# A softmax kernel: the first chunk's store split into a 512-byte head and the rest

## The chip, the cores and the metric

The kernel runs on one core of one Trainium2 chip. The metric is the device time of one execution in microseconds. Before the change it is 161.81 us, the median of three runs (161.65 to 161.95).

## The reference

A softmax with temperature 0.5 over the last dimension of a float32 tensor of 16 x 1024 x 512:

```python
temp = 0.5
x_scaled = x / temp
x_max = np.max(x_scaled, axis=-1, keepdims=True)
exp_x = np.exp(x_scaled - x_max)
return exp_x / np.sum(exp_x, axis=-1, keepdims=True)
```

33.55 MB are read and 33.55 MB are written; there is no matrix product.

## The kernel before

The 16384 rows are cut into 8 chunks of 2048 rows. A chunk is a tile `xt` of 128 partitions x 16 rows x 512 values, so each partition holds 16 neighbouring rows, one contiguous run of 32768 bytes in memory. All work on a chunk is done in place in this tile. There are six buffers (`BUFS`), so chunk 6 takes the buffer of chunk 0 and chunk 7 that of chunk 1, and their loads wait until those chunks are stored.

*Loads* (L61 to L69) are issued by SP on its queue, q1. Chunk 0 comes in two parts (rows 0 to 3, then 4 to 15), chunks 1 to 6 whole, and of chunk 7 the first 15 rows. The loads of chunks 0 to 5 go out one after the other at the start; those of 6 and 7 wait for a store. The last row of chunk 7 is loaded by POOL (L88 to L100, queue q0) after an exponential of chunk 5.

*Blocks* are what the engines work on: chunk 0 in three blocks (rows 0 to 3, 4 to 7, 8 to 15), chunk 7 in two halves, the others whole; eleven in all. For each block:
- `shift` (L71 to L81): DVE takes the negated maximum of each row (L77) and doubles it as a bias (L81);
- `exponentials` (L102 to L117): ACT computes exp(2x + bias) for one row of every partition per instruction (L108) and sums it up on the way;
- `scale_vector` (L120 to L131): DVE takes the reciprocals (L125) and multiplies the first 7/8 of the block's rows (L127);
- `scale_scalar` (L133 to L142): ACT multiplies the other eighth, row by row (L138);
- `store` (L144 to L152): when a chunk's last block is scaled, ACT issues one DMA of the whole chunk on its queue, q10 (L148). The table `STORES` has one whole store per chunk.

The order is written out by hand (L154 to L172), with a manual schedule. In step i, ACT runs the exponentials of block i+1, then DVE and ACT scale block i, then DVE shifts block i+2, then ACT issues the store. For block 3 (chunk 1) two of its 16 exponentials are kept back and run after the store that stands before them on ACT, which is chunk 0's store (L159, L172). The names of the DMAs are collected in `finished`; a last instruction on SP (L174) waits for them.

Below, load 5 or store 0 is that of chunk 5 or 0.

Of the kernel before, what the change touches and what calls it, by code (L numbers as in the profile page):

```python
# [1 line left out]

# [4 lines left out]


@with_exitstack
def kernel(  # L10
    ctx: ExitStack,
    tc: tile.TileContext,
    x: bass.AP,
    out: bass.AP,
):
    nc = tc.nc
    fp32 = mybir.dt.float32
    P = nc.NUM_PARTITIONS
    AX = mybir.AxisListType.X
    EXP = mybir.ActivationFunctionType.Exp  # L20
    COPY = mybir.ActivationFunctionType.Copy
    MAX = mybir.AluOpType.max

    D = x.shape[-1]
    xf = x.flatten_outer_dims()
    of = out.flatten_outer_dims()
    N = xf.shape[0]

    G = 16
    C = N // (P * G)
    assert C * P * G == N
    xr = xf.rearrange("(c p g) d -> c p g d", p=P, g=G)
    outr = of.rearrange("(c p g) d -> c p g d", p=P, g=G)
    WHOLE = [(0, G)]
    LOADS = [[(0, 4), (4, G)]] + [WHOLE] * 6 + [[(0, G - 1)]]
    BLOCKS = [[(0, 4), (4, 8), (8, G)]] + [WHOLE] * 6 + [[(0, 8), (8, G)]]
    STORES = [WHOLE] * 8  # L40
    BMAX = 16
    BUFS = 6

    data = ctx.enter_context(tc.tile_pool(name="data", bufs=BUFS))
    stats = ctx.enter_context(tc.tile_pool(name="stats", bufs=6))

    ctx.enter_context(tc.manual_schedule())


    warm = stats.tile([P, 1], fp32, name="warm", bufs=1)  # L50
    nc.vector.memset(warm, 0.0)  # L51
    nc.scalar.activation(out=warm, in_=warm, func=EXP)  # L52

    chunks = {}
    blocks = [(c, lo, hi) for c in range(C) for lo, hi in BLOCKS[c]]
    n = len(blocks)
    biases, sums, recips = {}, {}, {}

    finished = []

    def load(c):  # L61
        if c < BUFS:
            chunks[c] = data.tile([P, G, D], fp32, name="xt")
        else:
            chunks[c] = chunks[c - BUFS]
        xt = chunks[c]
        for lo, hi in LOADS[c]:
            part = nc.sync.dma_start(out=xt[:, lo:hi, :], in_=xr[c][:, lo:hi, :])  # L68
            finished.append(part.ins.name)  # L69

    def shift(i):  # L71
        c, lo, hi = blocks[i]
        if c not in chunks:
            load(c)
        b = hi - lo
        negmax = stats.tile([P, BMAX], fp32, name="negmax")
        nc.vector.tensor_reduce(  # L77
            negmax[:, 0:b], chunks[c][:, lo:hi, :], axis=AX, op=MAX, negate=True
        )
        biases[i] = stats.tile([P, BMAX], fp32, name="bias")  # L80
        nc.vector.tensor_scalar_mul(biases[i][:, 0:b], negmax[:, 0:b], 2.0)  # L81

    def load_last_row(signal):  # L88
        seen = stats.tile([P, 1], fp32, name="seen", bufs=1)
        copied = nc.gpsimd.tensor_copy(out=seen, in_=signal)  # L90
        finished.append(copied.ins.name)
        c = C - 1
        halves = "p (h d) -> p h d"
        to = chunks[c - BUFS][:, G - 1, :].rearrange(halves, h=2)
        of_ = xr[c][:, G - 1, :].rearrange(halves, h=2)
        for p0, p1 in ((P - 2, P), (0, P - 2)):
            part = nc.gpsimd.dma_start(  # L97
                out=to[p0:p1], in_=of_[p0:p1], max_dma_last_dim=2 * D
            )
            finished.append(part.ins.name)  # L100

    def exponentials(i, rows):  # L102
        c, lo, hi = blocks[i]
        if i not in sums:
            sums[i] = stats.tile([P, BMAX], fp32, name="sums")
        for g in rows:
            row = chunks[c][:, lo + g, :]
            nc.scalar.activation(  # L108
                out=row,
                in_=row,  # L110
                func=EXP,
                bias=biases[i][:, g : g + 1],
                scale=2.0,
                accum_out=sums[i][:, g : g + 1],
            )
            if c == BUFS - 1 and g == 10:
                load_last_row(sums[i][:, g : g + 1])  # L117


    def scale_vector(i):  # L120
        c, lo, hi = blocks[i]
        b = hi - lo
        k = b - b // 8
        recips[i] = stats.tile([P, BMAX], fp32, name="recip")
        nc.vector.reciprocal(recips[i][:, 0:b], sums[i][:, 0:b])  # L125
        rows = chunks[c][:, lo : lo + k, :]
        last = nc.vector.tensor_mul(  # L127
            rows, rows, recips[i][:, 0:k].unsqueeze(2).broadcast_to((P, k, D))
        )
        if i == n - 1:  # L130
            finished.append(last.ins.name)  # L131

    def scale_scalar(i):  # L133
        c, lo, hi = blocks[i]
        b = hi - lo
        for g in range(b - b // 8, b):
            row = chunks[c][:, lo + g, :]
            last = nc.scalar.activation(  # L138
                out=row, in_=row, func=COPY, scale=recips[i][:, g : g + 1]
            )  # L140
            if i == n - 1:
                finished.append(last.ins.name)  # L142

    def store(i):  # L144
        c, _, end = blocks[i]
        for lo, hi in STORES[c]:
            if hi == end:
                part = nc.scalar.dma_start(  # L148
                    out=outr[c][:, lo:hi, :], in_=chunks[c][:, lo:hi, :]
                )  # L150
                if c < C - 1:
                    finished.append(part.ins.name)  # L152

    shift(0)  # L154
    shift(1)

    def rows(i):
        c, lo, hi = blocks[i]
        cut = hi - lo - (2 if c == 1 else 0)  # L159
        return range(cut), range(cut, hi - lo)  # L160

    exponentials(0, rows(0)[0])
    for i in range(n):
        if i + 1 < n:
            exponentials(i + 1, rows(i + 1)[0])
        scale_vector(i)
        scale_scalar(i)
        if i + 2 < n:
            shift(i + 2)
        store(i)  # L170
        if i + 1 < n:
            exponentials(i + 1, rows(i + 1)[1])  # L172

    seen = nc.sync.nop()  # L174
    info = mybir.DependencyInfo(
        mybir.DependencyClass.Sync, mybir.DependencyReason.DATA
    )
    for name in finished:
        tc.add_manual_dep(seen.ins, name, info, reason="leaves one wait for the end")


# [1 line left out]
_INS = ['x']  # L183
_OUTS = [((16, 1024, 512), 'float32')]


# [23 lines left out]
```

## Time and profile before

| What | us |
|---|---|
| median of three runs | 161.81 |
| span of the profiled execution | 160.5 |
| difference of the two, outside the span | 1.3 |
| DVE busy, 45 instructions | 134.6 |
| ACT busy, 273 instructions | 102.2 |
| POOL busy, 7 instructions | 1.9 |
| store, from issue to landing, median of 8 | 23.1 |
| load of a whole chunk, from issue to landing, median of 6 | 34.8 |

The profile is of one execution; its own time is its span and what lies around it, and it is not timed apart, so the difference above is taken against the median. The page names, for each engine, its busy time; then the span in 40 slices of 4.01 us, where a digit is a busy share in tenths and the row GB/s what the 16 DMA engines moved; then the DMA queues with packets, megabytes and share of the 16 engines' time; then the chain that ended last; then groups of instructions by line. A stage table gives the same figures for stretches that one chooses, and a timeline gives instructions one by one: start, duration, engine, line, operation, what is written and read, and in brackets the idle time before it and who ended it. "ACTq" is the sequencer of ACT issuing a DMA. The trace also holds one record per DMA packet: start, duration, bytes and queue.

### The profile page before, as it was taken

What the parts mean: (1) busy time and instruction counts of PE and PEld (TensorE: products, weight loads), DVE (VectorE), ACT (ScalarE), POOL (GpSimd) and SP (SyncE); (2) the same over time, 40 slices, a digit from 0 to 9 for tenths busy, and PEclk for the clock granted to TensorE, in tenths of its full rate; (3) what the DMA queues carried; (4) which work ended last, traced back from release to release, by engine and by line L of the source; (5) the groups of instructions that cost most, each with busy time, mean ns of one, the idle gap of its engine ahead of it and who ended that gap; (6) DMA issues with size and microseconds to landing.
All of it is one profiled execution on the core that took longest, in us unless ns stands there. A gap on an engine that the chain in (4) does not pass through costs nothing.

```text
span 160.5 us, 411 instructions
## 1 busy us (share of the span) xinstructions
DVE 134.6 (84%) x45; ACT 102.2 (64%) x273; POOL 1.9 (1%) x7
## 2 busy tenths in 40 slices
DVE  0607999999999999999999999999999999957000
ACT  3071549069989963998199909991899891790000
POOL 0000000000000000000000000030000000000000
DMA  5999999999989999999999999989999999999994
GB/s 184 470 408 498 400 392 457 457 392 402 506 269 425 490 392 400 506 400 392 490 425 392 474 434 392 490 383 483 422 450 400 400 465 441 392 457 449 400 441 204
DMA packets 2578, 67.13 MB, mean 418 GB/s; under 512 B 328, under 2 KB 328, under 8 KB 400
## 3 DMA queue, kind: packets, MB, share of 16 engines
q1 hardware_dynamic: 1296, 33.29, 49.3%
q10 hardware_dynamic: 1152, 33.55, 48.4%
q0 software_dynamic: 128, 0.26, 0.4%
q14 instruction: 2, 0.02, 0.0%
HBM read 33.55 MB, written 33.55 MB: 418 GB/s over the span
## 4 chain that ended last, share of the span: by engine, by line
DVE 75%; DMA 7%; issue 5%; ACT 3%; SPq 0%
DVE negmax L77 42%; DVE xt L127 31%; DMA xt<-in_x_dram 7%; ACT xt L108 3%; DVE bias L81 1%; DVE recip L125 1%; SPq L68 0%
## 5 line engine op out<-in xcount | busy, mean ns | idle before, releaser
L108 ACT ACTIVATE xt<-xt,bias 128x512 f32<-128x512 f32 x128 | 90.4, 708 | 41.5 <-DVE bias L81 40.6
L77 DVE TENSOR_REDUCE negmax<-xt 128x16 f32<-128x8192 f32 (+2 forms) x11 | 69.9, 6352 | 9.4 <-DMA xt<-in_x_dram 9.4
L127 DVE TENSOR_TENSOR xt<-xt,recip 128x7168 f32<-128x7168 f32 (+2 forms) x11 | 62.0, 5637 | 0.4
L108 ACT ACTIVATION_READ_ACCUMULATOR xt<-xt,bias 128x1 f32 x128 | 23.9, 187 | 0.0
L138 ACT ACTIVATE xt<-xt,recip 128x512 f32<-128x512 f32 x15 | 9.9, 706 | 0.0
L125 DVE RECIPROCAL recip<-sums 128x16 f32<-128x16 f32 (+2 forms) x11 | 2.4, 218 | 1.8 <-ACT xt L108 1.8
L81 DVE TENSOR_SCALAR bias<-negmax 128x16 f32<-128x16 f32 (+2 forms) x11 | 1.9, 173 | 0.4
L52 ACT ACT_TABLE_LOAD x1 | 1.3, 1283 | 0.7 <-PEq L194 0.7
L97 POOL DMA_DIRECT2D xt<-in_x_dram x2 | 1.5, 741 | 0.5 <-issue 0.5
L90 POOL COPY seen<-sums 128x1 f32<-128x1 f32 x1 | 0.2, 184 | 103.6 <-ACT xt L108 103.6
L51 DVE MEMSET warm<- 128x1 f32 x1 | 0.1, 59 | 0.8 <-PEq L194 0.8
L52 ACT ACTIVATE warm<-warm 128x1 f32<-128x1 f32 x1 | 0.2, 202 | 0.0
L194 POOL MEMSET const-float32-0.0<- 128x1 f32 x1 | 0.1, 93 | 0.2 <-issue 0.2
L194 POOL MEMSET const-bfloat16-1.0<- 128x1 bf16 x1 | 0.1, 95 | 0.0
L194 POOL MEMSET const-uint8-127<- 128x1 uint8 x1 | 0.1, 95 | 0.0
L194 POOL MEMSET const-float32-1.0<- 128x1 f32 x1 | 0.1, 93 | 0.0
## 6 DMA issues: line engine op xcount, KB each, us to landing
out_dram<-xt ACTq DMA_DIRECT2D x8, 4096.0 KB, 23.1
xt<-in_x_dram SPq DMA_DIRECT2D x6, 4096.0 KB, 34.8
xt<-in_x_dram SPq DMA_DIRECT2D x1, 3840.0 KB, 27.8
xt<-in_x_dram SPq DMA_DIRECT2D x1, 3072.0 KB, 11.6
xt<-in_x_dram SPq DMA_DIRECT2D x1, 1024.0 KB, 4.8
xt<-in_x_dram POOLq DMA_DIRECT2D x1, 252.0 KB, 15.4
xt<-in_x_dram POOLq DMA_DIRECT2D x1, 4.0 KB, 9.1
```

Of the source, the lines that this page charges most:

```text
L51: nc.vector.memset(warm, 0.0)
L52: nc.scalar.activation(out=warm, in_=warm, func=EXP)
L77: nc.vector.tensor_reduce(negmax[:, 0:b], chunks[c][:, lo:hi, :], axis=AX, op=MAX, negate=True)
L81: nc.vector.tensor_scalar_mul(biases[i][:, 0:b], negmax[:, 0:b], 2.0)
L90: copied = nc.gpsimd.tensor_copy(out=seen, in_=signal)
L97: part = nc.gpsimd.dma_start(out=to[p0:p1], in_=of_[p0:p1], max_dma_last_dim=2 * D)
L108: nc.scalar.activation(out=row, in_=row, func=EXP, bias=biases[i][:, g : g + 1], scale=2.0, accum_out=sums[i][:, g : g + 1],)
L125: nc.vector.reciprocal(recips[i][:, 0:b], sums[i][:, 0:b])
L127: last = nc.vector.tensor_mul(rows, rows, recips[i][:, 0:k].unsqueeze(2).broadcast_to((P, k, D)))
L138: last = nc.scalar.activation(out=row, in_=row, func=COPY, scale=recips[i][:, g : g + 1])
L194: nc = _bacc.Bacc("TRN2", target_bir_lowering=False, num_devices=1)
```

## The change

Chunk 0 is stored by two DMAs in place of one, both issued by ACT on the same queue: first 128 values (512 bytes) of each partition, then the other 8064 values (32256 bytes). The other stores keep their shape; they are written over a flattened view. `store` returns early for a block that doesn't end its chunk. Both DMAs of chunk 0 are added to `finished`, and the load of chunk 6, which takes chunk 0's buffer, has to wait for both.

```diff
-    STORES = [WHOLE] * 8
+    HEAD = D // 4
...
     def store(i):
         c, _, end = blocks[i]
-        for lo, hi in STORES[c]:
-            if hi == end:
-                part = nc.scalar.dma_start(
-                    out=outr[c][:, lo:hi, :], in_=chunks[c][:, lo:hi, :]
-                )
-                if c < C - 1:
-                    finished.append(part.ins.name)
+        if end < G:
+            return
+        flat = "p g d -> p (g d)"
+        to, of_ = outr[c].rearrange(flat), chunks[c].rearrange(flat)
+        for lo, hi in [(0, HEAD), (HEAD, G * D)] if c == 0 else [(0, G * D)]:
+            part = nc.scalar.dma_start(out=to[:, lo:hi], in_=of_[:, lo:hi])
+            if c < C - 1:
+                finished.append(part.ins.name)
```

On every engine but ACT the instructions stay the same and in the same order; on ACT one more DMA issue follows the first.

## The prediction

> **What bounds the kernel now.** I read the page from its DMA rows first, because the engine rows alone mislead: DVE is busy 84% and ACT 64% of the span, and the chain of waits puts 75% on DVE, yet the last thing to end is a store.
>
> ```profile
> DMA  5999999999989999999999999989999999999994
> GB/s 184 470 408 498 400 392 457 457 392 402 506 269 425 490 392 400 506 400 392 490 425 392 474 434 392 490 383 483 422 450 400 400 465 441 392 457 449 400 441 204
> ...
> q1 hardware_dynamic: 1296, 33.29, 49.3%
> q10 hardware_dynamic: 1152, 33.55, 48.4%
> q0 software_dynamic: 128, 0.26, 0.4%
> ```
>
> See that the three queues (q1 the loads of SP, q10 the stores of ACT, q0 POOL's) hold 98.1% of 16 DMA engines' time: 157.5 of 160.5 us. I put the trace's packet records in order engine by engine (each packet starts where another ended). A packet is one partition's run: 32768 bytes take 1213 ns, and the next starts after 1209 ns, whether the engine carries loads only (15 to 44 us), loads and stores in alternation (50 to 113) or stores only (121 to 159). Each engine has 128 such runs' worth of bytes, so 128 x 1.209 = 154.8 us that nothing hides. The first packet starts at 1.74, the last ends at 159.21 and the last landing is at 159.68. So about 2.7 us are lost, and they are in two places: up to 0.9 us per engine at the first load, and one stall in the middle. The stall is visible in the row above as the slice of 269 GB/s (44.1 to 48.2 us), and better in the stage table (columns: length, DVE, ACT, POOL, clock, DMA share, GB/s):
>
> ```profile
> 32.00:44.00 12.00, 11.93 (x5) 10.52 (x29) 0.00 (x0) 1.00 1.00 429
> 44.00:50.00 6.00, 5.93 (x4) 5.28 (x16) 0.00 (x0) 1.00 0.98 344
> 50.00:62.00 12.00, 12.00 (x2) 8.92 (x24) 0.00 (x0) 1.00 0.99 429
> ```
>
> See that the DMA share stays at 0.98 while the rate falls by 85 GB/s for 6 us: 0.51 MB, or 16 packets, one per engine. In the packet records it is a load packet that takes 2.2 to 2.5 us in place of 1.21, on 13 engines at 46.2 to 48.9, on the other three a packet earlier; the first store packet follows one load packet later (48.4 to 50.1). The excess is 0.77 to 1.28 us, about 1.15 on most engines, close to the 1.2 us of one store packet. What begins there is the first store:
>
> ```profile
> 44.10 0.37 ACTq L148 DMA_DIRECT2D out_dram<-xt  x1
> 44.52 0.72 ACT L108 ACTIVATE xt<-xt,bias 128x512 f32<-128x512 f32 x1 [0.45 <-ACT xt L138]
> ...
> 45.85 0.19 ACT L108 ACTIVATION_READ_ACCUMULATOR xt<-xt,bias 128x1 f32 x1
> 46.10 0.17 DVE L81 TENSOR_SCALAR bias<-negmax 128x16 f32<-128x16 f32 x1
> 46.18 0.24 DVE L125 RECIPROCAL recip<-sums 128x16 f32<-128x16 f32 x1
> ```
>
> The second limit is the compute chain. DVE has waited for nothing from 12.80 to 137; the last store can't be issued before it:
>
> ```profile
> 143.50 3.89 DVE L127 TENSOR_TENSOR xt<-xt,recip 128x3584 f32<-128x3584 f32 x1
> 147.48 0.34 ACTq L148 DMA_DIRECT2D out_dram<-xt  x1
> ```
>
> The engines finish store 6 between 148.47 and 149.51 and go on with store 7 at once. The earliest engine began it 0.99 us after the issue, which is as quick as the first load ever was (issue 0.743, first packets 1.737 to 2.335: 0.99 to 1.59 us). So compute runs only 0 to 1 us ahead of the DMA engines at the end. A shorter DMA stream is worth at most that.
>
> **The change, part by part.** Chunk 0's store is 128 packets of 32768 bytes, 8 per engine. After, 8 packets of 512 bytes per engine come first and then 8 of 32256, with one more 4-byte semaphore packet.
>
> *Packets.* A packet costs a fixed part and its bytes: 32768 bytes take 1213 ns, 30720 1138, 8192 309, 4096 beside the stores 159, 2048 84, 4 bytes 9. Per byte that is 1/27.3 ns, so 9 ns stay fixed. The bytes are the same, so 9 more packets add 9 x 9 = 0.08 us per engine; if every 512-byte write cost as much as a 2048-byte packet, 9 x 84 = 0.76. I take 0.08, because the fixed part holds from 4 to 32768 bytes. The Trainium skill speaks against the split: "DMA: Bandwidth & Descriptors", Rules for kernel authors, has small transfers joined and those under 64 KB as mostly overhead, and its table there gives 0.95 us for a 64 KB load, which would be the estimate +0.95 in place of +0.08; the trace's 2048-byte packets at 84 ns on POOL's queue disagree with that for a busy engine.
>
> *The stall.* No row shows a store ring that starts with a small packet, so its price is bounded: it falls from 1.15 us to the 0.03 of a 512-byte packet if it is the time of one first packet, and stays whole if it is a fixed price of the first write or comes back with the first large packet. For the first: POOL's queue starts at 109.7 to 111.3 beside both others with packets of 8 or 2048 bytes, and the packets around them keep their 1209 ns; when it grows to 4096 bytes (113.6) nothing stalls either, where 0.15 us would show. The two 8192-byte instruction packets (37.69 and 97.12) cost their engine 0.25 us beyond their own 0.3, which lies between. A price of 1.15 us fixed for any new ring is thus contradicted; one peculiar to stores is not. I take the fall, 1.1 us.
>
> *ACT's issue.* ACT issues one DMA more at 44.1. It took 0.37; SP's consecutive issues start 0.42 to 0.53 us apart, once 0.71. The two exponentials of chunk 1 kept behind the store (L172) end 0.42 later: 46.04 becomes 46.46. DVE's reciprocal at 46.18 needs their sums, and its cover was 0.14 us. So DVE slips 0.28 to 0.57 us; I take 0.3. As DVE never waits until 137, all of that reaches store 7: issue at 147.78 in place of 147.48. POOL's trigger (L90) slips with it, and its row (landed 120.95, wanted at 132.83) has 12 us to spare.
>
> *What the loads do.* Packets alternate between queues, so eight load packets pass beside the eight tiny ones: 8 x 1.21 = 9.7 us in which almost only loads move. Load 5, landed at 76.87 before, ends at 66 to 67. The large part of store 0 follows with the last loads and then alone, so it lands at about 73 against 68.59. SP's load 6 (L68), behind which load 7 and the final wait stand, now waits for both parts and goes out at 73 rather than 68.67. The engines have store 1 (issued 58.95) to work on meanwhile. Load 6 then shares with stores for 16 packets, 19.4 us, and lands at about 96 as before (96.29); it is wanted at 103.86. Load 7 (landed 115.78, wanted 120.48) waits for store 1, which lands near 87 as before. Nothing is late; cost 0, with 4.7 us of cover at the tightest.
>
> *The sum.* DMA alone: 0.08 - 1.1 = -1.0 us, so store 6 would end at 147.5 to 148.5. But store 7's packets can come only at 147.78 + 0.99 to 1.59 = 148.8 to 149.4, against 149.51 where the last engine began before. So the DMA engines idle at the end and the gain is 0.1 to 0.7 us; I take the middle, 0.4. The span goes from 160.5 to 160.1. What lies around the span is 161.81 - 160.51 = 1.3 us to the median, unchanged: **161.4 us**.
>
> **Rivals.**
> 1. *The stall stays whole, only later or at the same place* (a price of the first write, or of the first large store packet that then intrudes before the loads). For it: no small first packet of a store is on record, and the stalled packet is a load ahead of the store. Then +0.08, and DVE's 0.3 us stays under the 1 us of cover on the late engines: 161.9, from 161.8 to 162.2.
> 2. *The other side: the load queue runs dry and pays a stall of its own.* Between about 67 and 73 us q1 is empty, which it never was before its end; load 6 then enters beside a busy store queue with 32768-byte packets. If a ring's entry costs 1.15 us, it is paid at about 75 us. It decides as soon as load 5 ends before store 0 lands. With the first stall gone: 161.81 - 1.1 + 1.15 + 0.08 = 161.9; with the first stall whole: 161.81 + 1.15 + 0.08 = 163.0. For it: the instruction packets, which re-enter a ring and cost 0.25 us extra each time. Against it: POOL's loads enter free.
> 3. *The split doesn't do what it says*: the 32256 bytes, no round size, might be cut up further. The trace has 24576 and 30720 as one packet each, so I give this almost nothing; it would land near 162.2.
>
> **How the numbers follow.** Stall gone, entry of loads free (161.4; own range 160.9 to 161.75): 0.45. Stall whole (161.9): 0.25. One stall traded for another (161.9): 0.12. Both stalls (163.0): 0.13. Something else, the 0.76 of dear small packets among it: 0.05. The range 160.9 to 162.2 leaves out the two stalls and part of the rest. Within 0.2% (161.49 to 162.13) is about what a measurement of this kernel can tell from no change. Faster takes three quarters of the first case and a little of the others, 0.36; same the rest of the first, most of the second and two thirds of the third, 0.42; slower 0.22.
>
> **What would show it.** Right: the slice at 44 to 48 us back at 400 or more, DVE's reciprocal at about 46.5, load 5 landed at 65 to 68, load 6 issued near 73, the last store issued at 147.8 and its 8 packets per engine starting after a short idle time. Wrong: a dip of the rate at 56 to 60 us (the stall moved), one at 73 to 77 us (entry of the loads), small store packets of well over 30 ns, or DVE waiting for load 6 or 7.

## The result and the profile after

| | before | after |
|---|---|---|
| median of four runs, us | 161.88 (161.65 to 161.96) | 163.30 (162.89 to 163.53) |
| span, us | 160.1, the median of its later runs; the one of the profile shown has 160.5 | 161.25, the median of four; the one of the profile has 161.2 |
| time outside the span, us | 1.72 to 1.83 in its later runs | 2.02 to 2.09 |

The ratio is 1.0084, with a 95% interval from 1.0066 to 1.0101: the change makes the kernel slower by 1.4 us, where 161.4 us and a small gain had been forecast, and above the range. About 1.15 us of it lie in the span (161.25 - 160.1) and 0.27 outside it (2.05 - 1.78, the medians). Where the executions of a kernel below fall into two groups more than 1.5% apart, its ratio is made from the shorter group.

The DMA rows of the page after:

```profile
DMA  5999999999999799999999999999999999999994
GB/s 193 458 439 472 390 423 488 390 415 490 400 405 489 291 460 443 403 452 439 390 455 333 415 445 435 432 438 417 427 441 448 431 423 447 431 423 439 431 431 187
...
q1 hardware_dynamic: 1296, 33.29, 49.4%
q10 hardware_dynamic: 1296, 33.56, 48.3%
q0 software_dynamic: 128, 0.26, 0.4%
```

Before, the row GB/s had one low slice in the middle, 269 at 44 to 48 us. Now it has two: 291 at 52.4 to 56.4 us and 333 at 84.6 to 88.6. The 144 more packets on q10 (1296 in place of 1152) are the 128 pieces of 512 bytes and 16 semaphore packets. The stage table after (length, DVE, ACT, POOL, clock, DMA share, GB/s) shows the same:

```profile
44.00:50.00 6.00, 5.93 (x4) 5.39 (x15) 0.00 (x0) 1.00 1.03 444
50.00:56.00 6.00, 6.00 (x2) 6.00 (x18) 0.00 (x0) 1.00 0.96 352
...
80.00:92.00 12.00, 12.00 (x2) 11.97 (x34) 0.00 (x0) 1.00 0.99 390
92.00:104.00 12.00, 11.93 (x5) 8.02 (x23) 0.10 (x1) 1.00 1.00 431
```

and before had in the same stretch

```profile
80.00:92.00 12.00, 12.00 (x2) 12.00 (x34) 0.00 (x0) 1.00 0.99 429
```

So the first stall is not gone: the 44 to 50 us in which before moved 344 GB/s now move 444, and the stall stands at 50 to 56 with 352. And there is a second one at 80 to 92, where before has none: 39 GB/s less for 12 us are 0.47 MB, some 14 packets of 32 KB, nearly one for each of the 16 engines. DVE and ACT are as busy there as before; the clock is 1.00 throughout.

One DMA engine's packet records show what a stall is (start in us, L a load packet, S a store packet, 512 and 4 the bytes where it isn't about 32 KB, +n the ns that it takes beyond its usual time):

```
before  45.16L +842  47.21L  48.41S  49.62L  50.83S  52.04L  53.25S
after   48.30S512  48.33L  49.54S512  49.56L  50.77S512  50.79L4  50.80S512  50.82L +221
        52.25S4  52.26L +615  54.08L +290  55.58S  56.77L
before  82.29L  83.50S  84.71L  85.92S4  85.93L  87.14S  88.35L  89.56S
after   82.05S  83.26L  84.47S  85.68L +1080  87.97S4  87.97L  89.18S  90.39L
```

The eight pieces of 512 bytes (the row shows the last four) pass beside the loads at 27 ns each. Then, when the first large store packet is about to come, load packets take 1.1 us too long, as in before. The second stall is like it: on this engine one load packet, between the last large packet of store 1 (84.47; the 4 bytes at 87.97 are its semaphore) and the first of store 2 (89.18). On others the time is split over the two load packets that stand there.

ACT's timeline after holds a surprise of another kind:

```profile
39.66 0.70 ACT L108 ACTIVATE xt<-xt,bias 128x512 f32<-128x512 f32 x1
39.68 0.38 ACTq L151 DMA_DIRECT2D out_dram<-xt  x1
...
43.18 0.70 ACT L138 ACTIVATE xt<-xt,recip 128x512 f32<-128x512 f32 x1
43.91 0.34 ACTq L151 DMA_DIRECT2D out_dram<-xt  x1
44.30 0.72 ACT L108 ACTIVATE xt<-xt,bias 128x512 f32<-128x512 f32 x1 [0.42 <-ACT xt L138]
...
46.00 0.24 DVE L125 RECIPROCAL recip<-sums 128x16 f32<-128x16 f32 x1
...
147.30 0.34 ACTq L151 DMA_DIRECT2D out_dram<-xt  x1
```

The head goes out at 39.68, not at 44.1. It covers a part of row 0, which DVE scales; nothing that ACT has yet to compute is in it. So ACT's sequencer issues it while ACT is still at exponentials that stand ahead of it in the program, 4.2 us before the rest (43.91), which needs the row that ACT scales at 43.18. What the head reads doesn't set the moment 39.68 either: row 0 had been scaled at 17.5 us, and kernels below whose first DMA reads rows 0 to 7 (half) or 0 to 14 (early15) issue it at the same place, 0.02 to 0.03 us after ACT's tenth exponential of chunk 1 has started. Five of the activations that stand ahead of it had yet to start, and so it is in all eight profiles below in which the first store goes out early. The issue at 43.91 costs ACT what the one issue of before did: DVE's reciprocal (46.00) and the last store (147.30) come 0.18 us earlier than in the profile of before, but the last store of an unchanged copy (after2, below) comes at 147.49, as in before.

### The profile page after: what moved, and what is told of

Read it like the earlier page. It is cut to its first block, busy times and chain, and to the rows that moved or that the text cites. A ratio compares the mean times of both kernels' runs of the same rounds, so it can differ in the third digit from the quotient of the medians.

```text
span 161.2 us, 414 instructions
## 1 busy us (share of the span) xinstructions
DVE 134.6 (84%) x45; ACT 102.2 (63%) x273; POOL 1.9 (1%) x7
## 3 DMA queue, kind: packets, MB, share of 16 engines
q1 hardware_dynamic: 1296, 33.29, 49.4%
q10 hardware_dynamic: 1296, 33.56, 48.3%
## 4 chain that ended last, share of the span: by engine, by line
DVE 75%; DMA 7%; issue 5%; ACT 3%; SPq 0%
DVE negmax L77 42%; DVE xt L127 31%; DMA xt<-in_x_dram 7%; ACT xt L108 3%; DVE bias L81 1%; DVE recip L125 1%; SPq L68 0%
```

## The experiments

**The measure.** For each experiment I took from the packet records, engine by engine, the time from a packet's start to the next one's start less 9 ns and the bytes at 27.3 per ns, and summed it up over the packets that start in a stretch. The table has the mean of the 16 engines, "lost early" for 38 to 60 us, where the first stall is, and "lost later" for 60 to 126 us. The mean says where time is lost and not what the execution takes, since the slowest engine and the time outside the span count in that. The times are medians, the ratio is against runs of before beside them (161.78 to 161.97).

| kernel | first store DMA issued | lost early, us | lost later, us | time, us | ratio, 95% |
|---|---|---|---|---|---|
| before | 44.10 | 1.13 | 0.05 | 161.88 | |
| dry | 43.99 | 0.90 | 0.05 | 162.15 | 0.9994 to 1.0023 |
| load_split | 44.07 | 0.75 | 0.05 | 162.18 | 1.0007 to 1.0026 |
| tail_split | 44.08 | 0.85 | 0.02 | 162.36 | 1.0017 to 1.0042 |
| late_head | 44.10 | 0.70 | 0.23 | 162.30 | 1.0018 to 1.0043 |
| held_head | 44.14 | 1.09 | 0.05 | 162.53 | 1.0022 to 1.0054 |
| held_head2 | 44.03 | 0.87 | 0.09 | 162.29 | 1.0020 to 1.0044 |
| late_gap | 44.24 | 0.75 | 0.12 | 162.25 | 1.0018 to 1.0043 |
| half_late | 44.11 | 0.77 | 0.08 | 163.33 | 1.0058 to 1.0138 |
| after | 39.68 | 0.85 | 1.12 | 163.30 | 1.0066 to 1.0101 |
| after2 | 39.87 | 0.93 | 0.96 | 163.47 | 1.0047 to 1.0105 |
| after_dry | 39.74 | 1.05 | 0.97 | 163.30 | 1.0045 to 1.0104 |
| half | 39.82 | 0.86 | 0.91 | 163.39 | 1.0062 to 1.0107 |
| early15 | 39.81 | 1.14 | 0.16 | 162.94 | 1.0039 to 1.0088 |
| early_both | 39.37 | 0.80 | 0.55 | 163.60 | 1.0090 to 1.0124 |
| early_one | 39.24 | 0.97 | 0.99 | see there | 1.0056 to 1.0123 |
| early_whole | 39.24 | 1.09 | 1.20 | see there | 1.0047 to 1.0094 |

My first theory was rival 2 of the prediction: the loads run dry at about 72 us, because they run ahead beside the small pieces, and the return of the load queue costs a stall. Its rivals were the size of the packets, and the extra DMA as such.

**dry: the load queue empty, without the change.** The kernel before, with load 6 held until ACT has scaled its row of chunk 2:

```diff
+    held, scaled = [], {}
...
+            if c == BUFS:
+                held.append(part)
...
+            scaled[i] = last.ins.name
...
+    tc.add_manual_dep(held[0].ins, scaled[4], info, reason="holds load 6")
```

> The kernel before, with no head; load 6 is held on SP until ACT has scaled its rows of chunk 2 (about 75.5 us), so the load queue is empty for some 4 us. Theory A (a store packet of 32 KB costs each DMA engine one stall of about 1.1 us when it is first taken up beside loads, and the same once more after the load queue has run empty): the stall at 46 to 49 us stays, a second one of about 1.1 us appears within some 10 us of the re-entry of loads, at the next boundary between two stores; time 161.9 + 1.1 = 163.0. Theory B (the second stall in the changed kernel comes from the small packets or the odd size of 32256 bytes, not from the empty queue): no second stall, 161.9.

Load 6 went out at 75.46 in place of 68.67, and the load queue was empty from about 74.8 us (one engine: 76.4) to 79.3. The stage table of dry:

```profile
40.00:52.00 12.00, 11.93 (x4) 11.28 (x32) 0.00 (x0) 1.00 1.01 407
...
74.00:80.00 6.00, 5.93 (x4) 1.99 (x5) 0.00 (x0) 1.00 1.00 431
80.00:92.00 12.00, 12.00 (x2) 12.00 (x34) 0.00 (x0) 1.00 1.01 437
```

The first stall is there (407 GB/s over 40 to 52), and none after the loads' return: 437, the full rate. The time is that of before. An empty load queue that returns costs nothing by itself; the theory falls. held_head, below, says it once more for the changed kernel: its load 5 landed at 65.5 to 67.2 us, load 6 went out at 72.14, and no second stall followed.

**head_wet and wet: keep the loads from running dry.** The rest of store 0 (head_wet), or the whole of store 0 (wet), goes out as partitions 0 to 63 and 64 to 127, and load 6 likewise, so that its first half could start earlier.

```diff
+        first = [(0, P, 0, HEAD), (0, H, HEAD, G * D), (H, P, HEAD, G * D)]
+        for p0, p1, lo, hi in first if c == 0 else whole:
```

> The changed kernel with its head, but the other 32256 bytes are stored by two DMAs of 64 partitions each, and load 6 comes in two DMAs of the same halves, so that its first half goes out when the first half of the store has landed and the load queue never runs empty. Theory A: one stall only, at 52 to 56 us where the first large store packet comes; about 1.1 us less than the changed kernel, 162.0 to 162.3. Theory B: both stalls, 163.2 or more.

> The control for the run with head and halves: the same halves of store 0 and load 6 without the head. Both theories: one stall at 46 to 49 us, 161.9 to 162.2. If the head itself is worth anything, the run with the head is faster than this one; theory A says it is not (the stall has only moved, and 0.1 us of small packets is added).

Both were misjudged: 173.69 to 177.68 us (head_wet) and 172.1 to 183.44 (wet), 6 to 8% slower by their shorter executions (ratios 1.0768, 1.0723 to 1.0813, and 1.0663, 1.0612 to 1.0714). The stage table of wet:

```profile
60.00:100.00 40.00, 39.79 (x12) 28.36 (x77) 0.00 (x0) 1.00 1.01 366
```

Load packets that usually take 1.2 us took 1.7 to 2.1 us in the median between 75 and 100 us, while the halves of load 6 ran, and the rate was 366 GB/s for 40 us (430 in before), which buries a stall of 1 us. The two runs tell nothing of the question. The Trainium skill, "SBUF — State Buffer", Door 1, says that a transfer's rate hangs on how many of the 16 ports its partitions reach, and by its formula partitions 0 to 63 reach only half of them. The 366 GB/s agree in direction.

**half: smaller first packets.** Chunk 0 is stored as rows 0 to 7 and 8 to 15, 16 KB a packet, and load 6 is cut alike, so that each part has its own load behind it.

```diff
+    LOADS = [[(0, 4), (4, G)]] + [WHOLE] * 5 + [[(0, 8), (8, G)], [(0, G - 1)]]
...
+    STORES = [[(0, 8), (8, G)]] + [WHOLE] * 7
...
-            if hi == end:
+            if end == G:
```

Both parts thus stand in the program behind chunk 0's last block, but the first reads only rows that DVE scales and goes out at 39.82 us.

> The kernel before, with store 0 and load 6 in two DMAs of 8 rows each, so packets of 16384 bytes for store 0 and no empty load queue. Theory A with the stall as large as the store packet that is taken up: a stall of about 0.6 us per engine at the first packet, and a second of about 0.6 us when store 1 brings packets of 32768 bytes; together as before, 161.9 to 162.3. Rival (a fixed price of the first store): one stall of 1.1 us and none at store 1, the same time; rival (the size of the first packet alone counts, growth is free): one of 0.6, 161.4. The place and size of the stalls tell them apart.

The stage table of half:

```profile
40.00:46.00 6.00, 6.00 (x1) 5.54 (x15) 0.00 (x0) 1.00 0.95 360
46.00:52.00 6.00, 5.93 (x4) 5.73 (x17) 0.00 (x0) 1.00 1.00 421
52.00:58.00 6.00, 6.00 (x2) 6.00 (x18) 0.00 (x0) 1.00 1.05 453
80.00:92.00 12.00, 12.00 (x2) 12.00 (x34) 0.00 (x0) 1.00 1.00 429
...
98.00:110.00 12.00, 12.00 (x2) 10.74 (x30) 1.66 (x3) 1.00 0.99 396
```

The first stall is paid in full with packets of half the size: 0.86 us lost early, where half of before's would be 0.57. When the packets grow from 16 to 32 KB, with store 1, nothing stalls. But here too there is a second stall, at 98 to 110 us, and here too between two stores (2 and 3). So neither the size of the first packet nor its growth sets the price, and 512-byte pieces are not needed for the second stall.

**after2, late_head, tail_split, load_split: the repeat, the place of the small piece, and one more DMA elsewhere.** after2 is an unchanged copy of after. late_head and tail_split change only the list:

```diff
-        for lo, hi in [(0, HEAD), (HEAD, G * D)] if c == 0 else [(0, G * D)]:
+        for lo, hi in [(G * D - HEAD, G * D), (0, G * D - HEAD)] if c == 0 else [(0, G * D)]:
```

for late_head, where the small piece still goes first but is the end of row 15, which ACT scales; in tail_split the large one, `(0, G * D - HEAD)`, goes first and the small one, `(G * D - HEAD, G * D)`, behind it. load_split is before with one more DMA on the loads' side:

```diff
-    LOADS = [[(0, 4), (4, G)]] + [WHOLE] * 6 + [[(0, G - 1)]]
+    LOADS = [[(0, 4), (4, G)], WHOLE, [(0, 8), (8, G)]] + [WHOLE] * 4 + [[(0, G - 1)]]
```

> The changed kernel once more, on the same chip as the three that follow. The run with the empty load queue but no head showed no second stall, so theory A in its first form (loads that run dry cost a stall) has fallen. Theory C: the second stall at 84 to 90 us belongs to the kernel and stands at the same place, the boundary of stores 1 and 2: 163.3, about 1 us per DMA engine in that stretch. Theory D: it is an accident of one execution and stands elsewhere or nowhere in this profile, and the time is then made up of something else.

> The changed kernel, but the 512 bytes are the last of each partition in place of the first, still issued first. They need ACT's scaled row, so both DMAs of store 0 go out together at about 44 us, not one at 39.7 and one at 43.9. Theory C1 (the small packets let the loads run eight packets ahead, and that shifts the phase of loads and stores): as the changed kernel, 163.0 to 163.5, both stalls some microseconds later. Theory C2 (the early issue matters, or load 5's place in time): only one stall, about 162.2.

> Store 0 in the same two sizes in the other order: first 32256 bytes, then the last 512. The first stall should be where the kernel before has it, 45 to 50 us, about 1 us (its first packets are large). The small packets come after it and again let eight loads pass. Theory C1: a second stall of about 1 us at a later boundary of two stores, 163.0 to 163.5. If the small packets matter only as the first thing that a store queue meets: no second stall, 162.0 to 162.2.

> The kernel before with no change to the stores: load 2 comes in two DMAs of 8 rows. That is one DMA more, as in the changed kernel, with the same shift of the semaphores that the DMAs use (load 5 then goes out at 5.3 in place of 3.8 us) and the same longer program, but all of it is over before the first store. Theory C1: one stall at 45 to 50 us and a span as before (160.0 to 160.5), plus 0.25 us outside the span, 162.1. Rival E (the second stall comes with the extra DMA and its semaphores, wherever it is): a second stall, 163.3.

The stage table over 80 to 92 us tells the four apart. In after2 the second stall of after repeats at the same place, 393 GB/s:

```profile
80.00:92.00 12.00, 12.00 (x2) 12.00 (x34) 0.00 (x0) 1.00 0.98 393
```

In late_head the rate is 429:

```profile
80.00:92.00 12.00, 11.97 (x3) 12.00 (x34) 0.00 (x0) 1.00 1.00 429
```

In tail_split it is 437:

```profile
80.00:92.00 12.00, 11.97 (x3) 12.00 (x34) 0.00 (x0) 1.00 1.01 437
```

And in load_split too:

```profile
80.00:92.00 12.00, 12.00 (x2) 12.00 (x34) 0.00 (x0) 1.00 1.01 437
```

Three things follow. A small piece ahead of the large one isn't what brings the second stall, since late_head has it and loses 0.23 us later, on a few engines. One more DMA costs 0.2 to 0.3 us even where nothing else changes: load_split's span is 160.15 in the median, that of before 160.1, but 2.04 us lie outside it, not 1.79. A second one adds hardly more: half, with two more DMAs than before, has 2.09 outside. And what sets late_head apart from after is the time of the first issue: 44.1, not 39.7, since row 15 is scaled by ACT.

**held_head, half_late, early15, after_dry: is it the early issue?** held_head is after with the head held until ACT has scaled its rows of chunk 0:

```diff
+            held.append(part)
...
+    tc.add_manual_dep(held[0].ins, scaled[2], info, reason="holds the head")
```

half_late is half with the same line for its first part. early15 is after with `HEAD = (G - 1) * D`: fifteen rows in the first DMA, at 39.8, and one row in the second. after_dry is after with the hold on load 6 that dry has.

> The changed kernel with one difference: the 512-byte DMA also waits for ACT's scaled row of chunk 0, so both DMAs of store 0 go out at about 44 us. Theory F (the second stall follows from the early issue of the first part at 39.7 us, which brings the large packets in at the third load of a chunk rather than the sixth): no second stall, 162.3, as in the run with the last 512 bytes. Theory G (it belongs to the first 512 bytes of the partition, say to their addresses): 163.4.

> Store 0 and load 6 in halves of 8 rows as before, which gave two stalls of 0.85 us, but the first half of the store also waits for ACT's scaled row and goes out at 44 us. Theory F: one stall, span about 160.3 and 162.3 in all. Theory G': two parts of 16384 bytes have two stalls wherever they start, 163.4.

> Store 0 in the sizes 30720 and 2048 bytes: the first 15 rows, which DVE alone scales, go out early at about 39.8 us, and the last row at 43.9. No packet of 512 bytes, but an early entry of large packets at the second or third load of chunk 4. Theory F: two stalls, 163.0 to 163.5. If only small first packets do the harm: 162.2.

> The changed kernel with load 6 held until ACT has scaled its rows of chunk 2 (about 75.3 us in place of 72.1), so that the loads come back some three packets later against store 1. Theory F with the phase of loads and stores as the carrier: the second stall moves or goes, since the loads return in the phase that they had left (the first store packet of a chunk after the third load packet): 162.3. If the early entry alone decides, whatever the phase on return: still two stalls, 163.4.

ACT's timeline in held_head has both issues at 44.14:

```profile
44.14 0.86 ACTq L153 DMA_DIRECT2D out_dram<-xt  x2
45.05 0.72 ACT L109 ACTIVATE xt<-xt,bias 128x512 f32<-128x512 f32 x1 [0.94 <-ACT xt L139]
```

and its stage table one dip:

```profile
52.00:58.00 6.00, 6.00 (x2) 6.00 (x19) 0.00 (x0) 1.00 1.06 388
...
80.00:92.00 12.00, 11.97 (x3) 12.00 (x34) 0.00 (x0) 1.00 0.97 418
92.00:104.00 12.00, 11.93 (x4) 8.00 (x22) 0.00 (x0) 1.00 1.03 446
```

The same two DMAs with the same bytes, 4.4 us later: the first stall is there (388), the second is not (418 and then 446, 0.05 us lost later). The median falls from 163.30 to 162.53. The second stall thus comes with the early issue. half_late agrees in the records (0.91 lost later in half, 0.08 here), but not in the time: 163.33, that of half. In its profile three packets lose 1.5 us between them at 95 to 108 us, and the loads of one engine end at 115.4 where the others' end at about 111.6. That is another loss, which I did not follow up; for 16 KB packets the late issue is not shown to save any time.

after_dry has its two stalls; the second comes earlier, 0.13 us at 74 to 80, 0.54 at 80 to 84 and 0.22 at 84 to 90. So it is not tied to one packet of the loads. early15 is the exception: it goes out early, loses 1.14 us early and only 0.16 later. Its profiled execution is the shortest of four (spans 160.6 to 161.2). Its price in time, 1.1 us over before, is not accounted for by these two numbers.

**early_one, early_both, late_gap: the gap between the two DMAs, or the early entry alone?** In early_one and early_both DVE scales all eight rows of chunk 0's last block, so that ACT has none to scale and a whole store 0 (early_one, on before) or both DMAs (early_both, on after) can go out at 39.3:

```diff
-        k = b - b // 8
+        k = b if i == 2 else b - b // 8
...
-        for g in range(b - b // 8, b):
+        for g in range(b if i == 2 else b - b // 8, b):
```

late_gap is held_head with the rest issued 4.5 us behind the head, at 48.72, from within the exponentials of chunk 2.

> The kernel before, store 0 in one DMA, but DVE scales all eight rows of chunk 0's last block (one row more, 0.55 us), so that the store waits for no scaling by ACT and can go out at about 40 us. Theory F1 (entering early is enough for a second stall): two stalls, 163.2 to 163.6. Theory F2 (an early entry does no harm unless the store is in two DMAs that reach the queue 4 us apart): one stall, and only DVE's 0.55 us at the end, 162.0 to 162.4.

> The changed kernel with the same extra row on DVE, so that its two DMAs of store 0 go out together at about 40 us: small packets first, early, but without the 4 us between. Theory F1: two stalls, 163.4. Theory F2: one stall, 162.3 to 162.6.

> The changed kernel with the 512-byte DMA held to 44 us and the rest issued after three exponentials of chunk 2, at about 48.4 us: the same 4 us between the two, but late. Theory F1: no second stall, 162.3 to 162.6. Theory F2: two stalls, 163.4.

The stage table of early_both has 404 GB/s over 80 to 92 us:

```profile
80.00:92.00 12.00, 11.97 (x4) 11.80 (x33) 0.00 (x0) 1.00 0.97 404
```

and that of late_gap has 434:

```profile
80.00:92.00 12.00, 12.00 (x2) 12.00 (x34) 0.00 (x0) 1.00 1.01 434
```

A gap between the DMAs is thus not needed (early_both has none and loses 0.55 us later) and does not bring the stall (late_gap has it and loses 0.12). early_one's two short executions took 162.84 and 163.69 us, the others 167.55 and 168.01, the profiled one among them.

**early_whole and held_head2: once more, the two that decide.** early_whole is the same kernel as early_one, held_head2 the same as held_head.

> The kernel before, with DVE scaling all 8 rows of chunk 0's last block, so that chunk 0's whole store in one DMA goes out at 39.3 in place of 44.1: the same kernel as early_one, whose profiled execution was disturbed. DVE's extra row shifts the last store by about 0.5 us. If an early entry of the stores is enough for the second stall: two stalls of about 1 us per DMA engine, at 40 to 44 and at a later border between two stores, span 161.2 to 161.8, time 163.0 to 163.5. If it also needs the split in two: one stall at 40 to 44, the extra row as an idle time at the end, span 160.3 to 160.8, time 162.1 to 162.6.

> An unchanged copy of held_head: the head at 44.1 and not 39.7. If the entry at 39.7 is what brings the second stall: again one stall of 0.7 to 1.1 us per engine at 50 to 58 and none later, span 160.2 to 160.6, time about 162.5. If the second stall is there or not by chance: a second dip between 74 and 110 us, span above 161.

held_head2 has one stall, 0.87 us, and loses 0.09 later; 162.29 us. The absence repeats. early_whole took 162.44 to 163.56 us in three executions and 166.95 to 168.25 in four, and the ratio is made from the three. The profile is of one of the four, and shows why they are long. Its stage table:

```profile
40.00:46.00 6.00, 6.00 (x1) 4.80 (x14) 0.00 (x0) 1.00 1.02 366
...
80.00:92.00 12.00, 11.97 (x3) 11.98 (x34) 0.00 (x0) 1.00 0.99 410
```

and DVE's timeline:

```profile
125.64 4.42 DVE L77 TENSOR_REDUCE negmax<-xt 128x8 f32<-128x4096 f32 x1 [4.29 <-DMA xt<-in_x_dram]
```

After the first stall (366) every engine loses time again. Fifteen of them lose 0.4 to 1.5 us between 60 and 126 us, in the mean 0.93, not all at one place; the sixteenth loses 5.2 us and ends its loads at 124.0, where the others end at 117 to 118, and DVE waits 4.29 us for load 7. This is one whole store in one DMA, as in before, only issued at 39.24 in place of 44.10, so the split may not be needed for the later loss. But that is not shown for the executions of usual length: both profiles, this one and early_one's, are of long ones. The five short executions of the two have spans of 160.7 to 161.9 us, where before has 160.0 to 160.1 in the median and DVE's extra row was expected to add 0.5; that leaves room for a later loss in most of them and shows none.

**What the runs show together.** Nine profiles with the first store DMA at about 44 us lose 0.02 to 0.23 us per engine after 60 us. Six with it at 39.4 to 39.9 us, in executions of usual length, lose 0.55 to 1.12, with the one exception of early15 (0.16); the two long executions of early_one and early_whole lose 0.99 and 1.20. The cleanest comparison is that of after and held_head, each with a copy: the same DMAs and bytes, and only the head's issue moved, 1.12 and 0.96 us lost later against 0.05 and 0.09. So in the changed kernel the trigger of the second stall is shown: the head's issue 4 to 5 us sooner. That an early store always brings it is not shown (early15), nor that a late one always saves the time (half_late). What happens in the DMA engines to make them stall once more, some 40 to 60 us later, stays open. Ruled out as the only cause, each by a kernel that has the thing and no stall or the stall and not the thing: an empty load queue (dry, held_head), the small piece and its bytes (held_head, half), growing packets (half at store 1), the extra DMA (load_split), the gap (late_gap, early_both). In after and half the second stall lies between the last packet of one store and the first of the next; that is an observation and no cause. A kernel faster than before was not found.

## Why the prediction was wrong, point by point

- *What bounds the kernel.* Right: after has both hardware queues at 97.7% of the DMA engines' time, and what its span gains is time lost in packet records.
- *Packets.* Right: 27 ns for a packet of 512 bytes, 0.08 us in all, against 28 ns. The 0.95 us that the Trainium skill's table in "DMA: Bandwidth & Descriptors", Bandwidth, has for a 64 KB load issued by GpSimd shows nowhere in the DMA engines' time.
- *The stall.* This step failed: "I take the fall, 1.1 us". The bound it had from POOL's queue, that small packets enter free, was right, and so was the guess that the head would. But the price is not that of the store queue's first packet. It is paid at the first large one, which came some 7 us later than before (55.6 in place of 48.4 on the engine shown): 0.85 us in after, where a fall by 1.1 to almost nothing had been forecast, and 0.70 to 1.14 in all seventeen profiles of the table, with 16 KB packets as with 32 KB. That is rival 1, at 52 to 56 us; the prediction had looked for it at 56 to 60.
- *ACT's issue.* It failed in its place: I counted the head's issue at 44.1, behind ACT's work, because it stands there in the program. It waits for none of ACT's work that it doesn't read, and ran 4.2 us ahead, with five of ACT's activations before it yet to start. Where the small piece goes out at 44.1 as I had it, the slip comes in the forecast size: in held_head the two issues take 0.86 us, the next exponential starts at 45.05 (before 44.52), and the last store goes out at 147.91 in place of 147.48. In after it is 147.30 (147.49 in after2), so the 0.3 us was not paid there, and that limit on the gain doesn't bind.
- *What the loads do.* Roughly right: load 5 landed at 69.1 to 70.8 (66 to 67 expected; the head came sooner, beside load 4 too; in held_head, with the head at 44.14, it landed at 65.5 to 67.2), the rest of store 0 at 71.2 to 72.0, load 6 went out at 72.06 (73) and landed at 95.6 to 97.1 (96). DVE waits for loads only where it did:

```profile
DVE negmax L77 <- DMA xt<-in_x_dram: 9.3, 2, 4.8
```

- *The sum.* It lacked two terms. One is the later loss, +1.07 us (1.12 less 0.05). Rival 2 had its size and its sign, and with the first stall whole its time, 163.0; its mechanism, the empty load queue, is contradicted by dry and by held_head, so that its number came near by coincidence. The other is the time outside the span, which I took as unchanged: +0.27 (load_split, where only a load is split, has 0.25 more too). With the small packets, 0.27 + 1.07 + 0.08 = 1.42, which is what was measured, if the first stall counts as unchanged. In the two profiles shown it is 0.28 smaller after, but in before's relatives (dry, load_split, tail_split) it was 0.75 to 0.90, so that 1.13 is on the high side for before.
- *The time around the span.* I took 1.3 us from the span of one execution and the median of others. Executions of before whose span and time are both known have 1.72 to 1.83: the profiled one was longer than the median run. The difference that I forecast is made against the median and doesn't suffer from it; but the execution on which I measured the stall was 0.4 us longer than the median one, and its stall, 1.13 us, longer than that of before's relatives.
- *The range.* It ended at 162.2 and left out "both stalls", 163.0, with a chance of 0.13. That case came nearest, by its size and not by its mechanism. The early entry that brings the second stall had been in no view.

## What to carry to other kernels

Before you count a DMA's issue where it stands in the program, ask what it reads: an issue that needs nothing of its own engine's pending work can go out microseconds ahead of it (4.2 here), and everything that follows from when a queue starts changes with it. A loss seen at the start of a stream need not belong to the first packet; move it, halve it and delay it before you cost its removal as a gain. And when the DMA engines are the bound, read a change by the time lost per packet over the whole run, since a second loss can stand 40 us and more behind the edit.

## What had not been expected of the hardware

- The first large store packets that enter beside loads cost the DMA engines once 0.70 to 1.14 us in the mean of the 16, with 16 KB as with 32 KB; eight 512-byte packets entered at 27 ns each, and did not pay it off.
- Stores issued at 39.4 to 39.9 us in place of 44.1 were followed by a further loss of 0.55 to 1.12 us per engine after 60 us, in five profiles of six (two more, of long executions, lost 0.99 and 1.20), in three kernels (after, half and after_dry) as a clear stall between two stores' packets or at the loads' return. Why is open.
- A kernel with one more DMA, whether on SP's queue or ACT's, lies 2.04 to 2.09 us outside its span in the median, one with two more (half, half_late) 2.06 to 2.09, one with the old number 1.75 to 1.79.
- ACT's sequencer issued a DMA 4.2 us ahead of its place among ACT's own instructions: in all eight profiles with an early first store, five activations that stand before it had yet to start.
- Transfers of 64 partitions brought the DMA engines from 430 to 366 GB/s over 40 us.
